# One step of a diffusion backbone layer on one Trainium2 core: the 16 by 16 triangular inverses of the scan move from VectorE to GpSimd

## The chip, the core and the metric

The kernel runs as one program on one core of a Trainium2 chip. Its time is the device time in microseconds (us). Before the change it is 2394.75 us, the median of three runs that lie between 2390.08 and 2395.71 us. The engines are written as in the profile: PE is TensorE, DVE is VectorE, ACT is ScalarE, POOL is GpSimd, SP is SyncE; a q behind a name is that engine's instruction queue, in which DMAs are issued.

## What is computed

One layer of a hybrid model over 1024 latent tokens and 256 context tokens of width 1024, all in float32. The token mixer has three branches: neighbourhood attention over an 8 by 16 window and the context, a bidirectional RWKV-7 scan, and a gated MLP over chunks of 128 positions. They are merged by sigmoid gates; then come an output projection, a normalisation, a SwiGLU feed-forward part and a second normalisation. The change touches only the scan:

```
def step(S, inp):
    r_t, w_t, k_t, v_t, kk_t, a_t = inp
    s_kk = jnp.einsum('...vk,...k->...v', S, kk_t)
    S = (S * w_t[..., None, :] - s_kk[..., :, None] * (kk_t * a_t)[..., None, :]
         + v_t[..., :, None] * k_t[..., None, :])
    return S, (jnp.einsum('...vk,...k->...v', S, r_t) if emit else None)
```

It runs in two directions, for 8 heads of width 64, over 1280 positions; the state after the context seeds the latent part.

## The kernel before

The scan is done in chunks of 64 positions. Inside a chunk the recurrence is a linear system with a 64 by 64 unit triangular matrix for each head and direction, and the kernel inverts these matrices ahead of the steps that use them.

The unit of work is called a block here. Block m (0 to 19, the list `L` at line 582) is one pair of heads, both directions, and four chunks of each, so that 16 matrices are inverted at once. Neighbouring blocks belong to two different pairs of heads; the state goes from block m to block m + 2. `rwkv_run` prepares blocks 0 and 1, then for each m runs the four rounds of `step` of block m (lines 744 to 785) and prepares block m + 2.

`prep` (line 626) loads a block's inputs, takes the exponentials `E` (L638, three buffers, so that the buffer of block m is free when the steps of block m - 3 are done; POOL sets the ones in it, L637), builds the factors `BK`, `KKe` and `KKo` on DVE (L643 to L649) and on POOL (L652, L653), multiplies them on PE (L662), transposes `BK` (L665) and masks the result into the triangular matrices `G` on DVE (L672, L673).

`invert` (line 691) writes `G` to DRAM (L697) and reads back the four 16 by 16 diagonal blocks of each of the 16 matrices, so that 64 small matrices lie on 64 partitions (`z`, tile gz, L699). POOL sets `Dm`, the first half of the tile DD, to the identity (L702, L703). Then comes the substitution: 15 steps, each a product into `tmp` (tile dtmp, L707) and an addition into `Dm` (L709). Step q works on 15 - q rows of q + 1 values, 15 to 64 values on each partition, 45.3 on average, and each instruction needs the one before it. L710 copies the transposed result into the second half of DD. DD goes to DRAM (L712) and comes back spread over 128 partitions as `Dc` (L714). DVE spreads it into block diagonal matrices `Db` and `Dt` (L730), and PE and DVE build the full inverse `X` from them in four rounds (tile ho, L725; L734, L739). gz, DD and dtmp have one buffer each. The steps of block m need its `X` at L763.

PE also has work that fills gaps: 28 projections of the input (`filling`, L543), 48 products of 128 by 512 each, written as L223, L224 and L225 with the tile d. They belong to the gates and to the queries and are called after the scan in the program. Here they are named fill products. Their weights are split on ACT (L211) and, in four pieces each, on POOL (L215).

No order is written out by hand around the change. All instructions are put into the queues of their engines when the program is built, by a scheduler that takes from the ready ones by priority, with a planned duration for each instruction. Each engine runs its queue strictly in order. So a fill product stands in PE's queue where the plan saw a gap, whether or not there is one on the chip.

Of the kernel before, what the change touches and what calls it, by code (L numbers as in the profile page):

```python
# [12 lines left out]
ALU = mybir.AluOpType  # L13
# [46 lines left out]
class Kern:  # L60
# [630 lines left out]
    def invert(self, jobs):  # L691
        nc, c = self.nc, self.c
        gs = self.dr.tile([16, 4160], F32, name="gs", tag="gs", bufs=2)
        for d, J in enumerate(jobs):
            for h in range(2):
                dst = bass.AP(gs.tensor, gs.offset + (8 * d + h) * 4160, [[64, 64], [8320, 4], [1, 64]])
                nc.scalar.dma_start(dst, J["G"][64 * h:64 * h + 64])  # L697
        z = self.T([64, 16, 16], "gz", 1)
        nc.sync.dma_start(z, bass.AP(gs.tensor, gs.offset, [[1040, 64], [64, 16], [1, 16]]))  # L699
        DD, tmp = self.T([64, 2, 16, 16], "DD", 1), self.T([64, 64], "dtmp", 1)  # L700
        Dm = DD[:, 0]
        nc.gpsimd.memset(Dm, 0.0)  # L702
        nc.gpsimd.memset(Dm.rearrange("p a b -> p (a b)")[:, 0:256:17], 1.0)  # L703
        for q in range(15):
            n, w = 15 - q, q + 1
            t = tmp[:, 0:n * w].rearrange("p (a b) -> p a b", b=w)
            nc.vector.tensor_tensor(t, z[:, q, q + 1:16].unsqueeze(2).to_broadcast([64, n, w]),  # L707
                                    Dm[:, q, 0:w].unsqueeze(1).to_broadcast([64, n, w]), ALU.mult)
            nc.vector.tensor_tensor(Dm[:, q + 1:16, 0:w], Dm[:, q + 1:16, 0:w], t, ALU.add)  # L709
        nc.vector.tensor_copy(DD[:, 1], Dm.rearrange("p a b -> p b a"))  # L710
        ds = self.dr.tile([2, 64, 256], F32, name="ds", tag="ds", bufs=2)
        nc.sync.dma_start(ds.rearrange("x p f -> p x f"), DD.rearrange("p x a b -> p x (a b)"))  # L712
        Dc = self.T([P, 16, 16], "Dc", 1)
        nc.sync.dma_start(Dc, bass.AP(ds.tensor, ds.offset, [[16, P], [2048, 16], [1, 16]]))  # L714
        bmb = c["bm"].rearrange("p (b t) -> p b t", t=16).unsqueeze(1).to_broadcast([P, 8, 4, 16])

        def blk(x):
            return x.rearrange("p u (b t) -> p u b t", t=16)

        def each(e, f):  # L720
            for u in range(8):
                for z in (0, 64):
                    q = slice(z, z + 64)
                    w, x = f(q, u)
                    nc.tensor.matmul(e[q, u, :], w, x, start=True, stop=True)  # L725

        Db, Dt, ET = (self.T([P, 8, 64], n, 1) for n in ("Db", "Dt", "ET"))
        X = self.T([P, 8, 64], "X", 2)
        for o, q in ((Db, 0), (Dt, 8)):
            nc.vector.tensor_tensor(blk(o), Dc[:, q:q + 8, :].unsqueeze(2).to_broadcast([P, 8, 4, 16]), bmb, ALU.mult)  # L730
        nc.scalar.activation(X, Dt, AF.Copy)
        e = self.ps.tile([P, 8, 64], F32, name="ho", tag="ho", bufs=1)
        each(e, lambda q, u: (jobs[u // 4]["G"][q, u % 4, :], Db[q, u, :]))
        nc.vector.tensor_tensor(ET, e, c["om"].unsqueeze(1).to_broadcast([P, 8, 64]), ALU.mult)  # L734
        src = Dt
        for t0 in (16, 32, 48):
            e = self.ps.tile([P, 8, 64 - t0], F32, name="ho", tag="ho", bufs=1)
            each(e, lambda q, u: (ET[q, u, :], src[q, u, t0:64]))
            nc.vector.tensor_tensor(X[:, :, t0:64], e, Dt[:, :, t0:64], ALU.add)  # L739
            src = X  # L740
        for d, J in enumerate(jobs):
            J["X"] = X[:, 4 * d:4 * d + 4]
# [724 lines left out]
```

## Time and profile before

| what | value |
|---|---|
| median of three runs | 2394.75 us |
| the profiled execution's own time | 2394.73 us |
| its span in the profile | 2392.9 us |
| PE busy | 2253.3 us, 94% |
| DVE busy | 1531.1 us, 64% |
| ACT busy | 895.3 us, 37% |
| POOL busy | 683.8 us, 29% |
| the scan, first L757 to last steps | 525.1 to 1097.5 us |
| DVE, ACT, POOL busy in it | 435.08, 233.28, 104.72 us |

The profile is one execution. A group's row has its line, engine, operation, output<-inputs, shape and count; then busy time and the mean of one in ns; then the idle time of the engine before it with what ended it. A timeline row has start, duration, engine, line and tiles, and in brackets the idle time before it. A wait row has total, times and longest. Each 64 by 64 product shows as two PE records, so x32 in a PE row are 16 products of the program.

### The profile page before, as it was taken

Reading aid. Unit: us, or ns where it says so; the run is one execution under the profiler, and the core shown is the slowest. Engines: PE = TensorE matmul, PEld = TensorE weight load, DVE = VectorE, ACT = ScalarE, POOL = GpSimd, SP = SyncE. Lnnn points to the kernel's source line nnn. Section 1 sums busy time; section 2 is a strip of 40 time slices with the busy share of each in tenths; the row PEclk is TensorE's granted clock in tenths of the full one; section 3 lists DMA queues with packets and bytes.
Section 4 is the critical chain, followed back from the end, with each engine's and each line's share of the span. In section 5 each row is a group of like instructions: output and inputs, shape, how many; then the busy total and the mean of one; then the engine's idle time right before and its main releaser. Section 6 shows DMA issues by size and latency. Waiting matters only on the chain.

```text
span 2392.9 us, 40066 instructions
## 1 busy us (share of the span) xinstructions
PE 2253.3 (94%) x15352; PEld 1790.2 (75%) x15352; DVE 1531.1 (64%) x3054; ACT 895.3 (37%) x1697; POOL 683.8 (29%) x708
## 2 busy tenths in 40 slices
PE   5899999998899998999999989999799999999997
PEld 4778888876677766667777768777588888877886
DVE  8885445437778777771676745686775555555835
ACT  4432425333344434343454532332533333332421
POOL 6221213441111121112312230333444333325402
PEclk9999999999999999899999999999799999999999
DMA  7676444545344444433865666464122222246541
GB/s 248 211 234 173 143 137 148 191 134 121 98 108 113 111 109 106 102 79 91 214 171 141 162 213 218 144 215 138 62 90 87 85 90 82 80 161 248 172 158 53
DMA packets 291861, 337.50 MB, mean 141 GB/s; under 512 B 140082, under 2 KB 210994, under 8 KB 291668
## 3 DMA queue, kind: packets, MB, share of 16 engines
q1 hardware_dynamic: 224548, 240.91, 34.6%
q10 hardware_dynamic: 54608, 51.40, 7.2%
q0 software_dynamic: 12512, 42.62, 4.9%
q8 instruction: 121, 1.98, 0.4%
q14 instruction: 72, 0.59, 0.1%
HBM read 248.85 MB, written 85.99 MB: 140 GB/s over the span
## 4 chain that ended last, share of the span: by engine, by line
PE 68%; DVE 16%; DMA 5%; issue 4%; ACT 4%; POOL 3%; SPq 0%; ACTq 0%; DVEq 0%; POOLq 0%
PE d L225 13%; PE d L223 13%; PE d L224 13%; PE ho L725 3%; PE pv L909 3%; PE d L1028 3%; PE d L1029 3%; PE d L1027 3%; PE gr L662 2%; PE pt L895 2%; DVE w L243 1%; DVE junk L243 1%; PE sc L771 1%; DVE DD L709 1%; DVE dtmp L707 1%
## 5 line engine op out<-in xcount | busy, mean ns | idle before, releaser
L225 PE MATMUL d<-hh,wl 128*128 128x512 f32 x1056 | 429.5, 407 | 0.0
L223 PE MATMUL d<-hh,wh 128*128 128x512 f32 x1056 | 428.8, 406 | 0.0
L224 PE MATMUL d<-hl,wh 128*128 128x512 f32 x1056 | 428.3, 406 | 0.0
L225 PEld LDWEIGHTS d<-hh,wl 128*128 128x128 f32 x1056 | 201.8, 191 | 46.8 <-issue 5.4
L224 PEld LDWEIGHTS d<-hl,wh 128*128 128x128 f32 x1056 | 201.7, 191 | 44.2 <-issue 3.4
L223 PEld LDWEIGHTS d<-hh,wh 128*128 128x128 f32 x1056 | 201.4, 191 | 43.2 <-issue 3.6
L215 DVE TENSOR_TENSOR wl<-wr,wh 128x1024 fp32r<-128x1024 f32 x51 | 65.0, 1274 | 159.8 <-ACT wh L211 111.5
L211 ACT ACTIVATE wh<-wr 128x1024 fp32r<-128x1024 f32 x79 | 83.5, 1057 | 191.8 <-PE d L224 149.1
L215 POOL TENSOR_TENSOR wl<-wr,wh 128x256 fp32r<-128x256 f32 x112 | 86.6, 803 | 225.3 <-ACT wh L211 211.7
L240 DVE TENSOR_TENSOR o<-wr,o 128x1024 fp32r<-128x1024 f32 (+1 forms) x64 | 92.5, 1447 | 20.3 <-ACT o L237 19.9
L1028 PE MATMUL d<-dl,ah 128*128 128x512 f32 x252 | 98.4, 391 | 2.8 <-DVE dl L240 2.8
L1029 PE MATMUL d<-dh,al 128*128 128x512 f32 x252 | 98.3, 390 | 0.1
L1027 PE MATMUL d<-dh,ah 128*128 128x512 f32 x252 | 98.2, 390 | 0.1
L237 ACT ACTIVATE o<-wr 128x1024 fp32r<-128x1024 f32 (+1 forms) x64 | 59.2, 926 | 100.0 <-PE d L224 73.9
L909 PE MATMUL pv<-pT,V 128*64 128x128 f32 (+2 forms) x640 | 93.5, 285 | 0.0
L240 DVE TENSOR_TENSOR al<-ar,ah 128x512 fp32r<-128x512 f32 x42 | 42.1, 1020 | 78.6 <-ACT ah L237 78.6
L1022 POOL TENSOR_TENSOR wl<-wr,wh 128x1024 fp32r<-128x1024 f32 x16 | 42.9, 2690 | 169.4 <-DVE wr L1020 124.3
L1255 POOL TENSOR_TENSOR act<-act 128x512 f32<-128x512 f32 x22 | 29.6, 1348 | 194.0 <-issue 160.1
L781 ACT ACTIVATE rv<-sc,E 64x64 f32<-64x64 f32 x152 | 38.9, 303 | 123.1 <-DVE rv L779 112.8
L662 PE MATMUL gr<-KKo,BK 64*128 64x128 f32 (+1 forms) x320 | 61.5, 313 | 24.3 <-DVE KKo L649 21.2
L909 PEld LDWEIGHTS pv<-pT,V 128*64 128x64 f32 (+2 forms) x640 | 69.2, 139 | 18.2 <-issue 13.0
L707 DVE TENSOR_TENSOR dtmp<-gz,DD 64x15 f32<-64x15 f32 (+2 forms) x300 | 70.6, 235 | 16.5 <-DMA gz<-gs 7.7
(397 smaller groups left out, 5878.7 us busy)
## 6 DMA issues: line engine op xcount, KB each, us to landing
wr<-wgu SPq DMA_DIRECT2D x45, 512.0 KB
dr<-wdn SPq DMA_DIRECT2D x42, 512.0 KB
wa<-wada SPq DMA_DIRECT2D x32, 512.0 KB
wr<-win SPq DMA_DIRECT2D x31, 512.0 KB
wr<-win ACTq DMA_DIRECT2D x28, 512.0 KB
s_gt<-stg ACTq DMA_DIRECT2D x48, 256.0 KB
wr<-wbr SPq DMA_DIRECT2D x24, 512.0 KB
g<-s_gt SPq DMA_DIRECT2D x48, 256.0 KB
```

Source lines behind the costliest of these rows:

```text
L211: nc.scalar.activation(hi[:, :n], raw[:, :n], AF.Copy)
L215: (lo_eng or self.lo_eng).tensor_tensor(lo[:, q], raw[:, q], hi[:, q].bitcast(F32), ALU.subtract)
L223: nc.tensor.matmul(ps, w, xh, start=first and k == 0, stop=False)
L224: nc.tensor.matmul(ps, w, xl, start=False, stop=False)
L225: self.last = nc.tensor.matmul(ps, lo[:, P * k:P * k + P], xh, start=False, stop=last and k == n - 1)
L240: (lo_eng or nc.vector).tensor_tensor(lo, src, hi.bitcast(F32), ALU.subtract)
L662: prev = nc.tensor.matmul(o[:, u, 0:W], x, y, start=True, stop=True)
L707: nc.vector.tensor_tensor(t, z[:, q, q + 1:16].unsqueeze(2).to_broadcast([64, n, w]), Dm[:, q, 0:w].unsqueeze(1).to_broadcast([64, n, w]), ...
L909: nc.tensor.matmul(o, V[0:k, vt, 64 * e:64 * e + 64], pt[0:k, i, :], start=(i == 0), stop=(i == len(cols) - 1))
L1027: nc.tensor.matmul(ps, xh, wh, start=first, stop=False)
L1028: nc.tensor.matmul(ps, xh, wl, start=False, stop=False)
L1029: nc.tensor.matmul(ps, xl, wh, start=False, stop=last)
```

## The change

The 15 products, the 15 additions and the transposed copy of each block go to POOL instead of DVE. Nothing else is edited.

```diff
@@ -704,10 +704,10 @@
         for q in range(15):
             n, w = 15 - q, q + 1
             t = tmp[:, 0:n * w].rearrange("p (a b) -> p a b", b=w)
-            nc.vector.tensor_tensor(t, z[:, q, q + 1:16].unsqueeze(2).to_broadcast([64, n, w]),
+            nc.gpsimd.tensor_tensor(t, z[:, q, q + 1:16].unsqueeze(2).to_broadcast([64, n, w]),
                                     Dm[:, q, 0:w].unsqueeze(1).to_broadcast([64, n, w]), ALU.mult)
-            nc.vector.tensor_tensor(Dm[:, q + 1:16, 0:w], Dm[:, q + 1:16, 0:w], t, ALU.add)
-        nc.vector.tensor_copy(DD[:, 1], Dm.rearrange("p a b -> p b a"))
+            nc.gpsimd.tensor_tensor(Dm[:, q + 1:16, 0:w], Dm[:, q + 1:16, 0:w], t, ALU.add)
+        nc.gpsimd.tensor_copy(DD[:, 1], Dm.rearrange("p a b -> p b a"))
         ds = self.dr.tile([2, 64, 256], F32, name="ds", tag="ds", bufs=2)
         nc.sync.dma_start(ds.rearrange("x p f -> p x f"), DD.rearrange("p x a b -> p x (a b)"))
         Dc = self.T([P, 16, 16], "Dc", 1)
```

The scheduler plans the whole program anew, and the queues of all engines change in the scan. POOL's queue around block 13, before: the preparation of block 13 (KKe_3984 to KKo_3989), a weight of a fill projection (wl), then the identity of block 13.

```order
297 L637 MEMSET E 128x4 x2
298 L652 TENSOR_TENSOR KKe_3984<-E,rl 64x4x64
299 L653 TENSOR_TENSOR KKo_3985<-E,rl 64x4x64
300 L652 TENSOR_TENSOR KKe_3988<-E,rl 64x4x64
301 L653 TENSOR_TENSOR KKo_3989<-E,rl 64x4x64
302 L215 TENSOR_TENSOR wl<-wr,wh 128x256 x4
303 L702 MEMSET DD 64x256
304 L703 MEMSET DD 64x16
```

POOL's queue now, from the identity of block 13 on; KKe_3992 to KKo_3997 and the E ahead of them are the preparation of block 14.

```order
710 L702 MEMSET DD 64x256
711 L703 MEMSET DD 64x16
712 L637 MEMSET E 128x4 x2
713 L707 TENSOR_TENSOR dtmp<-gz,DD 64x15
714 L709 TENSOR_TENSOR DD<-DD,dtmp 64x15
715 L707 TENSOR_TENSOR dtmp<-gz,DD 64x28
716 L652 TENSOR_TENSOR KKe_3992<-E,rl 64x4x64
717 L709 TENSOR_TENSOR DD<-DD,dtmp 64x14x2
718 L653 TENSOR_TENSOR KKo_3993<-E,rl 64x4x64
719 L707 TENSOR_TENSOR dtmp<-gz,DD 64x39
720 L652 TENSOR_TENSOR KKe_3996<-E,rl 64x4x64
721 L709 TENSOR_TENSOR DD<-DD,dtmp 64x13x3
```

The substitution of block 13 now stands behind the memset of E for block 14, and four instructions of that block's preparation stand inside it.

PE's queue before, from the last transposes of block 14's preparation to the first product of block 13 that needs `Db`.

```order
3514 L665 MATMUL gr<-c_ident,BK 128x128 x4
3515 L225 MATMUL d<-hh_577,wl 128x512
3516 L223 MATMUL d<-hh_626,wh 128x512
3517 L224 MATMUL d<-hl_627,wh 128x512
3518 L763 MATMUL sc<-rb_4000,X 64x64 x4
3519 L225 MATMUL d<-hh_626,wl 128x512
3520 L223 MATMUL d<-hh_251,wh 128x512
3521 L224 MATMUL d<-hl_252,wh 128x512
3522 L225 MATMUL d<-hh_251,wl 128x512
3523 L223 MATMUL d<-hh_290,wh 128x512
3524 L224 MATMUL d<-hl_291,wh 128x512
3525 L725 MATMUL ho<-Db,G 64x64 x16
```

The same place in PE's queue now.

```order
3423 L665 MATMUL gr<-c_ident,BK 128x128 x3
3424 L223 MATMUL d<-hh_290,wh 128x512
3425 L224 MATMUL d<-hl_291,wh 128x512
3426 L225 MATMUL d<-hh_290,wl 128x512
3427 L223 MATMUL d<-hh_341,wh 128x512
3428 L224 MATMUL d<-hl_342,wh 128x512
3429 L725 MATMUL ho<-Db,G 64x64 x16
```

Five fill products and no step product stand there now, where nine fill products and four step products stood. Counted over the whole queue, 768 fill products stand between the first L757 and the last L775 of the scan before, and 641 now; behind the attention's last product, 232 before and 350 now.

## The prediction

> **What bounds the kernel now.** I read the page first, for the chain that ended last.
>
> ```profile
> PE 68%; DVE 16%; DMA 5%; issue 4%; ACT 4%; POOL 3%; SPq 0%; ACTq 0%; DVEq 0%; POOLq 0%
> L707 DVE TENSOR_TENSOR dtmp<-gz,DD 64x15 f32<-64x15 f32 (+2 forms) x300 | 70.6, 235 | 16.5 <-DMA gz<-gs 7.7
> ```
>
> PE leads, and the substitution takes DVE some 141 us in all (L709 is a twin of L707). Next, busy time by stage, for the scan and for the end of the fill behind the attention.
>
> ```profile
> core 0: us, PE busy (x) PEld busy (x) DVE busy (x) ACT busy (x) POOL busy (x), PEclk, DMA share, GB/s
> 525.10:1097.50 572.40, 527.85 (x6965) 396.58 (x6966) 435.08 (x1335) 233.28 (x709) 104.72 (x208) 0.95 0.43 105
> 1397.20:1447.00 49.80, 45.03 (x198) 34.82 (x197) 13.16 (x16) 13.06 (x20) 16.84 (x15) 0.97 0.71 244
> ```
>
> PE looks full in the scan, but a matmul's record overlaps the next, so busy is not work. What PE waits for at the first round of the inverse (L725) says more.
>
> ```profile
>   DVE Db L730: 16.3, 19
> ```
>
> In 19 of 20 blocks PE stands there, 0.86 us each, until `Db` comes: the work planned ahead of L725 just fails to cover the inverse's latency. So I follow one block, number 13, on the timelines of PE, DVE and POOL.
>
> ```profile
> 879.44 0.66 PE L665 MATMUL gr<-c_ident,BK 128*128 128x128 f32 x4
> 890.10 0.17 DVE L707 TENSOR_TENSOR dtmp<-gz,DD 64x15 f32<-64x15 f32 x1 [0.39 <-DMA gz<-gs]
> 895.03 0.15 POOL L637 MEMSET E<- 128x4 f32 x2 [10.90 <-ACT rv L781]
> 896.25 0.68 POOL L653 TENSOR_TENSOR KKo<-E,rl 64x256 f32<-64x256 f32 x1
> 896.29 0.72 DVE L707 TENSOR_TENSOR dtmp<-gz,DD 64x64 f32<-64x64 f32 x1
> 904.76 0.37 DVE L710 COPY DD<-DD 64x256 f32<-64x256 f32 x1
> 913.02 1.15 PE L725 MATMUL ho<-Db,G 64*64 64x64 f32 x32 [0.33 <-DVE Db L730]
> 924.42 0.21 DVE L707 TENSOR_TENSOR dtmp<-gz,DD 64x64 f32<-64x64 f32 x1
> ```
>
> From the end of the transposes (880.1) to L725 (913.0) pass 32.9 us; 15.0 of them, 890.1 to 905.1, are substitution and copy. Their own work on DVE is 7.4 us (30 x 0.235 + 0.37); the rest is other DVE work that stands between. The substitution of a block, first product to end of copy, averages 16.2 us over the 20 blocks; these are the ends of the first and of the last.
>
> ```profile
> 532.47 0.17 DVE L707 TENSOR_TENSOR dtmp<-gz,DD 64x15 f32<-64x15 f32 x1
> 545.86 0.37 DVE L710 COPY DD<-DD 64x256 f32<-64x256 f32 x1
> 1068.91 0.15 DVE L707 TENSOR_TENSOR dtmp<-gz,DD 64x15 f32<-64x15 f32 x1
> 1079.13 0.39 DVE L710 COPY DD<-DD 64x256 f32<-64x256 f32 x1
> ```
>
> **The substitution on POOL.** No row shows this form on POOL. The nearest are a product of one element, of 256, a copy, and the gap before L653.
>
> ```profile
> L1370 POOL TENSOR_TENSOR st<-st 128x1 f32<-128x1 f32 x7 | 1.4, 194 | 0.5
> L652 POOL TENSOR_TENSOR KKe<-E,rl 64x256 f32<-64x256 f32 x32 | 22.6, 705 | 24.7 <-ACT E L638 16.3 <-ACT ub L764 4.5 <-DMA rl<-s_r 2.3
> L653 POOL TENSOR_TENSOR KKo<-E,rl 64x256 f32<-64x256 f32 x32 | 23.4, 732 | 2.3
> L571 POOL COPY KKe<-c_ident 64x256 f32<-64x256 f32 x6 | 2.4, 394 | 0.2
> ```
>
> L653's undisturbed 0.68 gives (0.68 - 0.194) / 255 = 1.9 ns an element, so an average instruction of 45.3 elements takes 0.28 us, and with a gap of 2.3 / 32 = 0.07 it costs 0.35. Bounds are 0.19 and 0.70, the two rows; I take 0.35, on the line between them. Thirty make 10.6 us, the copy 0.46, together 11.1. Four things are added or taken:
>
> - POOL's queue has 23 of L652/L653 and 5 of L215 inside substitutions, at some 0.76 us: 1.1 us a block.
> - At a head like block 13's the substitution waits for `E`: the memset ran at 895.03, 4.9 us after the data were there. Seven heads stand like this; I take 2 us for each, 0.7 a block (0 to 5).
> - POOL and DVE hold each other up. The 64-element product takes 0.21 us alone (924.42) and 0.72 beside POOL's L653 (896.29). After the change the DVE operations with two inputs in SBUF meet the substitution:
>
> ```profile
> L649 DVE TENSOR_TENSOR KKo<-E,kkl 64x256 f32<-64x256 f32 x40 | 23.2, 579 | 1.2
> L648 DVE TENSOR_TENSOR KKe<-E,kkl 64x256 f32<-64x256 f32 x40 | 22.3, 557 | 12.9 <-ACT E L638 10.9 <-issue 1.1 <-POOL E L637 0.8
> L646 DVE SCALAR_TENSOR_TENSOR BK<-bb,le 128x256 f32<-128x256 f32 x40 | 18.9, 472 | 0.6 <-DMA bb<-s_bb 0.5
> L643 DVE TENSOR_TENSOR BK<-kd,le 128x256 f32<-128x256 f32 x20 | 9.3, 467 | 0.7 <-DMA kd<-s_kd 0.5
> L645 DVE TENSOR_TENSOR BK<-kd,le 128x256 f32<-128x256 f32 x20 | 8.8, 442 | 0.2
> L730 DVE TENSOR_TENSOR Db<-Dc,c_bm 128x512 f32<-128x512 f32 x20 | 13.8, 688 | 13.1 <-DMA Dc<-ds 13.0
> L730 DVE TENSOR_TENSOR Dt<-Dc,c_bm 128x512 f32<-128x512 f32 x20 | 13.7, 683 | 0.0
> ```
>
> Their sum is 110 us, 5.5 a block; a substitution fills 12 of a block's 28.6 us (572.4 / 20), so 2.3 meet it, and half of that, 1.2, holds it up (0 to 5.5).
> - `Db` no longer queues behind another block's substitution: 0.3 less.
>
> That is 11.1 + 1.1 + 0.7 + 1.2 = 14.1 against 16.2, and 0.3: the latency falls by **2.4 us** (5.4 with nothing in the way).
>
> Behind a substitution that waits stand the next block's L652/L653 and the weights of L215 in POOL's queue, and PE's L662 and L225 wait for those. I cost this at nothing, since the same late inverse holds PE at L725 a little later anyway; where that doesn't cover it, four of L652/L653 are 4 x 0.75 = 3 us for each of the seven heads, 21 us.
>
> [...]
>
> **The cover in PE's queue.** The spacing of fill products comes from a run of 57.
>
> ```profile
> 1419.67 0.39 PE L223 MATMUL d<-hh,wh 128*128 128x512 f32 x1
> 1432.49 0.39 PE L225 MATMUL d<-hh,wl 128*128 128x512 f32 x1
> ```
>
> 12.82 us / 56 = 0.229 us. With it, 0.07 for a product of L725 (1.15 / 16), 0.165 for a transpose (0.66 / 4), and an estimated 0.10 to 0.15 for the small products of the steps and of L662 between these, the work between a block's last transpose and its L725 falls from 26.4 to 20.0 us on average (block 13: 27.8 to 19.8). At the scan's clock of 0.95 that is **6.7 us less cover**, while the latency falls by 2.4: PE stands 4.3 us longer for each block's inverse. Where the wait of the block before lies inside the same stretch it counts for both. That is so in 9 of 20 blocks of the new queue, so a block pays 4.3 / 1.45 = 2.97, and 20 blocks **59 us**.
>
> **The sum.** In the scan:
> - 127 fill products fewer (768 to 641): 127 x 0.229 / 0.95 = 30.6 us less work.
> - 59 us more waiting for the inverse.
> - The steps' DVE operations (L759, L765, L779) lose the substitution from their queue. PE's waits for their results:
>
> ```profile
> PEld sc L757 <- ACT rv L781: 13.7, 25, 1.7
> PEld sc L771 <- DVE ub L765: 11.7, 21, 2.5
> PEld sc L763 <- ACT rb L760: 11.6, 24, 1.4
> PE sc L757 <- ACT rv L781: 6.2, 11, 1.5
> ```
>
> They make 43 us; I take a quarter off, 11 us (0 to 43), since longer waits for the inverse hide the rest.
>
> So the scan goes from 572.4 to 572.4 - 30.6 + 59 - 11 = 590. Behind the attention 118 fill products more (232 to 350) at 0.229 cost 27 us, uncovered: PE is busy 45 of 49.8 us there with nothing but fill. The other 9 lie under the attention; I cost them at nothing, and at 2 us without that cover. DMAs, memsets and tiles stay as they are. In all 17.4 + 27 = **+44 us**. The profiled execution took 2394.73 us, as good as the median, so the forecast is **2439 us**. About 0.3%, 7 us, is what a measurement of this kernel can tell from no change.
>
> **The rivals.**
>
> *The scan gains what the plan expects.* The substitution runs on POOL undisturbed (latency 5.4 us less) and three quarters of the 43 us go. For it speaks that DVE loses a third of its work in the scan; against it, the instructions inside POOL's substitutions. Waits grow by (6.7 - 5.4) / 1.45 x 20 = 18: -30.6 + 18 - 32 + 27 = -18, **2377 us**, faster. It decides if substitution and copy stay near 11 us. Chance 0.14.
>
> *Work only moves.* Latency as there, the steps' gain as in my sum: -30.6 + 18 - 11 + 27 = +3, **2398 us**, no change that can be told. For it speaks that the number of PE's instructions doesn't change and the 27 us are paid in any case; against it the same as above. Chance 0.13.
>
> [...] All 5.5 us of the DVE operations hold up each substitution, and the ten operations on the way wait some 0.28 us each for POOL: the latency rises by 5.5 - 1.2 + 2.8 - 2.4 = 4.7. Waits grow by (6.7 + 4.7) / 1.45 x 20 = 157: -30.6 + 157 - 11 + 27 = +142, **2537 us**. For it speaks the 0.72 beside 0.21; against it, that only part of these operations falls into a substitution. [...] Chance 0.06.
>
> My own case has 0.67. That the change isn't made is no rival: POOL's queue shows the chain.
>
> **Range and chances.** My case's bounds: a latency that falls by 4 us (half of the additions gone) gives 37 us of waits, +22; one that falls by 0.3, for long waits behind `E`, gives 88, +73, and without the steps' gain +84. Reaching into the other cases until 2 in 10 are left out gives 2388 to 2485. Faster 0.14, same 0.13, slower 0.73.
>
> **What would show it.** In the profile after: L707 and L709 on POOL near 0.28 us, with 0.07 between; a block's substitution with copy near 14 us; PE's wait at L725 for `Db` several times 16.3 us; the scan near 590 us; the fill behind the attention near 77 us (49.8 + 27). The forecast is wrong if the wait at L725 stays near 16 us, or if the scan gets shorter by more than 27 us.

## The result, and the profile after

The changed kernel takes 2451.61 us, median of four runs (2435.70 to 2460.36), beside 2392.41 us for four runs of the kernel before: a ratio on record of 1.0232, with an interval of 1.0202 to 1.0262 (the two medians alone give 1.0247). The profiled execution is the fastest of the four, 2435.70 us; its granted clock has a mean of 0.967, and that of the other three 0.954 to 0.958. Against the profiled execution of before (2394.73 us) it is 41.0 us longer.

On the page, the substitution is on POOL now; these rows stand beside the row of L707 shown of before.

```profile
L707 POOL TENSOR_TENSOR dtmp<-gz,DD 64x15 f32<-64x15 f32 (+2 forms) x300 | 83.6, 279 | 97.2 <-DMA gz<-gs 75.9
L709 POOL TENSOR_TENSOR DD<-DD,dtmp 64x15 f32<-64x15 f32 (+2 forms) x300 | 87.2, 291 | 22.5
```

An instruction takes 0.285 us on the mean, and where none of them waits for gz the idle time ahead of one is (97.2 - 75.9 + 22.5) / 600 = 0.073 us. The copy, from the groups of POOL:

```profile
L710 POOL COPY DD<-DD 64x256 f32<-64x256 f32 x20 | 12.6, 632 | 1.3
```

Next the stages: scan, attention, and the fill products behind it. The rows give the stretch, its length, the busy time of PE, PE's weight loads, DVE, ACT and POOL, and the granted clock third from the end. First before, cut at the end of the last L775.

```profile
525.10:1118.60 593.50, 548.54 (x7162) 411.17 (x7161) 437.66 (x1344) 240.44 (x732) 108.13 (x214) 0.95 0.42 104
1118.60:1397.40 278.80, 268.94 (x1633) 213.29 (x1634) 183.14 (x567) 137.23 (x255) 66.85 (x49) 0.98 0.62 166
1397.40:1447.40 50.00, 45.23 (x198) 35.02 (x199) 13.36 (x16) 13.36 (x20) 16.84 (x15) 0.97 0.70 243
```

The same stages after:

```profile
524.80:1139.30 614.50, 517.58 (x7035) 395.57 (x7034) 307.24 (x724) 235.54 (x729) 280.08 (x824) 0.91 0.39 96
1139.30:1414.30 275.00, 267.55 (x1642) 212.42 (x1643) 179.74 (x567) 136.40 (x255) 68.65 (x53) 0.99 0.63 171
1414.30:1487.60 73.30, 70.65 (x313) 55.72 (x314) 12.66 (x16) 18.33 (x27) 21.66 (x23) 1.00 0.56 199
```

The scan is 21.0 us longer, the attention 3.8 shorter, the tail 23.3 longer; with 0.5 elsewhere these are the 41.0 us. (The prediction cut the scan of before at 1097.5, inside the last block's inverse; the last step ends at 1118.6.) In the scan PE is busy 31.0 us less, and yet the scan is longer: PE stands more, and its clock is lower (0.91, where it was 0.95). What it stands for, in the table of waits (us in total, times, longest), before:

```profile
PE gr L662 <- DVE KKo L649: 21.2, 16, 2.3
PE sc L757 <- ACT rv L781: 6.5, 12, 1.5
PE ho L725 <- DVE Db L730: 5.9, 6, 2.6
PE sc L771 <- DVE ub L765: 4.2, 4, 2.1
PE sc L763 <- ACT rb L760: 3.5, 5, 1.2
PE gr L662 <- POOL KKo L653: 0.4, 1, 0.4
```

And after:

```profile
PE ho L725 <- DVE Db L730: 61.2, 15, 7.6
PE gr L662 <- POOL KKo L653: 24.4, 10, 6.1
PE gr L662 <- DVE KKo L649: 7.0, 7, 2.3
PE sc L763 <- ACT rb L760: 2.5, 2, 2.2
PE sc L757 <- ACT rv L781: 0.5, 2, 0.3
PE sc L771 <- DVE ub L765: 0.3, 1, 0.3
```

The wait for `Db` grew by 55.3 us, that at L662 by 24.0 - 14.2 = 9.8, and the steps' waits fell by 10.9: 54.2 us more. Block 13 again, whose rows stand in the prediction:

```profile
904.13 0.15 POOL L637 MEMSET E<- 128x4 f32 x2 [10.20 <-ACT rv L781]
904.23 0.21 POOL L707 TENSOR_TENSOR dtmp<-gz,DD 64x15 f32<-64x15 f32 x1
906.14 0.80 POOL L653 TENSOR_TENSOR KKo<-E,rl 64x256 f32<-64x256 f32 x1
916.18 0.55 PE L665 MATMUL gr<-c_ident,BK 128*128 128x128 f32 x3
917.82 0.60 POOL L710 COPY DD<-DD 64x256 f32<-64x256 f32 x1
924.00 0.69 DVE L730 TENSOR_TENSOR Db<-Dc,c_bm 128x512 f32<-128x512 f32 x1 [7.09 <-DMA Dc<-ds]
924.75 0.48 PE L725 MATMUL ho<-Db,G 64*64 64x64 f32 x4 [6.87 <-DVE Db L730]
```

The substitution starts late behind the memset of `E`, runs past the point at which PE has used up its queue (917.9), and PE stands 6.87 us where it stood 0.33.

**Scan, split in three.** For the experiments I split the scan, from the first L662 to the last L775, with the timeline of PE and the records of the granted clock: time without any product (idle), half of the busy time at half clock (an estimate of what the clock cost: in the traces of before and after, fill products follow each other every 0.43 us at half clock and every 0.23 at full clock), and the rest (PE's work at full clock). Each row is of one profiled execution: that of the changed kernel is the fastest of its four, that of e7 the slowest of its six (2466.77 us).

| kernel | scan | work | idle | clock |
|---|---|---|---|---|
| before | 605 | 526 | 48 | 32 |
| after | 625 | 485 | 100 | 41 |
| e5, engine alone | 611 | 522 | 42 | 47 |
| e6, plan alone | 634 | 483 | 83 | 68 |
| e1, engine and old order on PE | 716 | 518 | 117 | 80 |
| e2, DVE and new order on PE | 686 | 481 | 128 | 77 |
| e3b, short substitution, new plan | 558 | 488 | 45 | 25 |
| e7, products in the holes | 646 | 506 | 72 | 69 |
| e4b, L652 on DVE, new plan | 620 | 484 | 85 | 51 |
| e8, 18 operations on DVE, old plan | 633 | 524 | 60 | 50 |
| e11, engine alone, L652 on DVE | 574 | 528 | 34 | 11 |
| e12, L652 on DVE alone | 606 | 528 | 50 | 27 |

The work is that of the order: 518 to 528 us with the old one, 481 to 488 with the new (506 with e7's added 25). Everything else is idle time and clock.

### The profile page after: what moved, and what is told of

Same layout as the page of the kernel before. It is cut to its first block, busy times and chain, and to the rows that moved or that the text cites. A ratio compares the mean times of both kernels' runs of the same rounds, so it can differ in the third digit from the quotient of the medians.

```text
span 2433.7 us, 40095 instructions
## 1 busy us (share of the span) xinstructions
PE 2246.9 (92%) x15352; PEld 1795.4 (74%) x15352; DVE 1394.7 (57%) x2434; ACT 892.4 (37%) x1697; POOL 861.9 (35%) x1328
## 5 line engine op out<-in xcount | busy, mean ns | idle before, releaser
L215 DVE TENSOR_TENSOR wl<-wr,wh 128x1024 fp32r<-128x1024 f32 x51 | 64.9, 1273 | 190.1 <-ACT wh L211 141.7
L215 POOL TENSOR_TENSOR wl<-wr,wh 128x256 fp32r<-128x256 f32 x112 | 84.5, 782 | 241.9 <-ACT wh L211 165.8
L707 POOL TENSOR_TENSOR dtmp<-gz,DD 64x15 f32<-64x15 f32 (+2 forms) x300 | 83.6, 279 | 97.2 <-DMA gz<-gs 75.9
L709 POOL TENSOR_TENSOR DD<-DD,dtmp 64x15 f32<-64x15 f32 (+2 forms) x300 | 87.2, 291 | 22.5
L662 PE MATMUL gr<-KKo,BK 64*128 64x128 f32 (+1 forms) x320 | 61.4, 312 | 34.0 <-POOL KKo L653 24.4
L725 PE MATMUL ho<-Db,G 64*64 64x64 f32 x640 | 30.4, 263 | 61.3 <-DVE Db L730 61.2
```

What stands on the lines that cost most here:

```text
L215: (lo_eng or self.lo_eng).tensor_tensor(lo[:, q], raw[:, q], hi[:, q].bitcast(F32), ALU.subtract)
L707: nc.gpsimd.tensor_tensor(t, z[:, q, q + 1:16].unsqueeze(2).to_broadcast([64, n, w]), Dm[:, q, 0:w].unsqueeze(1).to_broadcast([64, n, w]), ...
L709: nc.gpsimd.tensor_tensor(Dm[:, q + 1:16, 0:w], Dm[:, q + 1:16, 0:w], t, ALU.add)
```

## The experiments

The theory: the loss is in the new plan, which puts 6.7 us less work ahead of L725 and moves 118 fill products behind the attention, while the latency falls by only 2 to 3 us. The main rival: the substitution on POOL costs by itself, through what it does to DVE and to POOL's queue. To part the two I held queues: at the end of the build each instruction of an engine gets an order-only edge (no wait) to the one ahead of it in the queue of the other kernel.

```diff
+def keep_order(tc, nc):
+    t = {i.name: i for i in nc.cur_bb.bb.instructions}
...
+            i = t.get(f"I-{at + int(d) + k}")
...
+                x = last.get(i.engine)
...
+                    tc.add_manual_dep(i, x.name, no, reason="keep_order")
+                last[i.engine] = i
```

**PE's order held, the rest planned anew.** Edit of e1 to the changed kernel, of e2 to the kernel before, with PE alone in the table:

```diff
         Kern(tc, aps).build()
+        pe_order(tc, nc)
```

> The changed kernel with all of PE's instructions held to the order they have in the kernel before (11778 places alike), substitution and copy on POOL; the other engines' orders are left to the scheduler. Theory (cover): the loss comes from PE's order, planned with 6.7 us less work ahead of L725 than before, while the latency fell by only 2 to 3 us. With the old cover back, PE's wait at L725 for Db falls from 122 us to below the 16 us of before, the tail behind the attention is 50 us again, and the steps keep their relief of some 11 us: 2392 - 11 - 10 = 2371 us, at most 2392. [...] Rival (tail): only the 118 fill products behind the attention cost, so 2452 - 27 = 2425 us.

> The kernel before, substitution and copy on DVE, with all of PE's instructions held to the order of the changed kernel. Theory (cover): the latency is that of before and the cover is 6.7 us shorter, so waits at L725 grow by 6.7 / 1.45 x 20 = 92 us over before, 31 us of fill leave the scan and 27 us come back behind the attention: 2392 + 92 - 31 + 27 = 2480 us, slower than the change itself. Rival (engine): with the chain back on DVE the time is back at 2392 to 2400 us. Rival (tail): 2392 + 27 = 2419 us.

Measured: e1 2498.5 us, ratio 1.0445 (1.0418 to 1.0472); e2 2507.1 us, 1.0494 (1.0456 to 1.0532). Both are slower than the change itself. For e1 the theory was wrong by over 100 us and the tail rival by 73; a cost of the substitution on POOL by itself, the main rival, was left standing. e2 came 27 us above the theory's 2480, and far above both of its rivals. PE's waits in e1:

```profile
PE gr L662 <- POOL KKo L653: 40.3, 10, 5.7
PE gr L662 <- DVE KKo L649: 33.1, 8, 7.3
```

`Db` is not among the late things any more; the next block's preparation is. In e1's POOL queue 22 of the 64 L652 and L653 stand inside a substitution and the others behind whole substitutions of 30 instructions, and a substitution at the queue's head waits for gz 216 us in all (75.9 in the changed kernel). Whether that was POOL or the new plan of the other queues, e1 cannot say, since holding PE had made the scheduler plan them anew.

**All five queues held.** The same edit with the instructions of all engines in the table: e5 is the engine without the plan, e6 the plan without the engine.

> The engine change without the new plan: substitution and copy on POOL, and the instructions of all five engines held to the order in which the kernel before issues them, the substitution merged into POOL's queue at the places that it has in the plan of before. It asks what held e1_chain_pool_old_order at 2498 us, where only PE was held and the other queues were planned anew (PE waited at L662 for KKo of L653 on POOL, 40 and 72 us). Theory (cover): with the old cover and old queues the shorter latency is left over: 2371 to 2392 us. Rival (POOL's queue): L652 and L653 of the next block stand behind a substitution that waits for gz, PE waits for them at L662, and the old cover makes this worse, not better, since in the old order L662 of the next block is ahead of L725: 2430 us or more, with waits at L662 over 60 us.

> The new plan without the engine change: substitution and copy on DVE, and the instructions of all five engines held to the order in which the changed kernel issues them, the substitution merged into DVE's queue at the places that it has in that plan. Theory (cover): PE's wait at L725 grows as in e2_chain_dve_new_order, which came to 2507 us with the other queues planned anew: 2480 to 2507 us. Rival: part of e2's time is from the other queues being planned anew around a PE order that did not suit them; with all queues as in the changed kernel it takes 2452 us like that, the engine makes no difference.

Measured: e5 2395.17 us, 0.9995 (0.9965 to 1.0025); e6 2446.90 us, 1.0208 (1.0168 to 1.0248). This separates them. The engine alone costs nothing that can be told, the plan alone costs 2.1%, against 2.3% for both. The rival of e5 fails (e1's time came from its other queues). In e6 the rival's 2452 us is the right one, and the theory's 2480 to 2507 is out. So the theory holds as to the cause, but not in two of its numbers. In e5 no gain is left over: first product to end of copy is 16.3 us a block on POOL with the old queues, where DVE took 16.2. POOL's other work inside it is 3.3 us a block, 2.1 of them L652 and L653; in the changed kernel it is 1.1. And in e6 it is 10.4 us on DVE, where the changed kernel takes 12.9 on POOL; yet the time is nearly the same. PE's waits in e6:

```profile
PE sc L771 <- DVE ub L765: 25.2, 18, 4.5
PE gr L662 <- DVE KKo L649: 23.2, 14, 4.0
PE sc L763 <- ACT rb L760: 11.6, 10, 2.3
PE sc L757 <- ACT rv L781: 7.1, 5, 2.7
```

`Db` is in time there (3 us of waiting), but the substitution stands in one piece in DVE's queue, ahead of the steps' operations, and PE stands for those. With less work planned in between, something is late; the engine decides which.

**Latency alone.** The substitution stops after 8 of 15 steps; e3 holds PE to the changed kernel's order, e3b all five engines.

```diff
-        for q in range(15):
+        for q in range(8):
```

> The changed kernel, PE in the changed kernel's own order, but the substitution stops after 8 of its 15 steps (16 POOL operations a block where there were 30; the last seven rows of every 16x16 inverse are left incomplete). Theory (cover): the latency falls by 14 x 0.36 = 5.0 us a block, and by the 1.45 of the prediction 5.0 / 1.45 x 20 = 69 us of waits go: 2452 - 69 = 2383 us, PE's wait at L725 near 50 us. Rival (engine by what it holds up, or tail): the wait at L725 only covers others, so that what goes there comes back at the steps or at L662: 2440 us or above.

> The changed kernel with the substitution stopped after 8 of its 15 steps (the last seven rows of every 16x16 inverse are left incomplete), and the instructions of all five engines held to the changed kernel's order, where e3_short_chain_new_order held PE alone. Theory (cover): 5.0 us less latency, 69 us less waiting: 2383 us, and no more waits at the steps than in the changed kernel. Rival (the steps take over): PE's waits at L763 and L771 grow as they did in e3 (18 to 57 us at L771), since the substitution was only the first of two late things: 2420 to 2435 us.

Measured: e3 2427.3 us, 1.0143 (1.0114 to 1.0172); e3b 2371.87 us, 0.9914 (0.9886 to 0.9941). With all queues held, time falls by as much as the theory's 69 us: (1.0232 - 0.9914) x 2392 = 76 us. The wait for `Db`:

```profile
PE ho L725 <- DVE Db L730: 21.2, 13, 2.9
```

The substitution became 5.7 us shorter (12.2 to 6.5, first to last of its operations), so a us of latency is worth 76 / 20 / 5.7 = 0.67 us a block, one part in 1.5. The prediction's 1 in 1.45 is another thing, since it counts waits alone. By the table the idle time fell by 55 us, one part in 2.1, of which the wait for `Db` is 40 us, and the clock gave 16 more. In e3 the freshly planned queues gave 24 us of waits at L771 and 12 at L763, and over two thirds of the gain were lost. The rival of e3b described e3's queues, not the kernel.

**Work in the holes.** Ten products ahead of L725 in the 11 blocks where PE stood longest, all queues held.

```diff
+        self.nb = getattr(self, "nb", -1) + 1
+        for _ in range(10 if self.nb in (1, 2, 3, 5, 7, 9, 12, 13, 15, 17, 19) else 0):
+            x = self.xs(0)[0][0]
+            nc.tensor.matmul(e.rearrange("p a b -> p (a b)"), x[:, 0:P], x, start=True, stop=True)
         each(e, lambda q, u: (jobs[u // 4]["G"][q, u % 4, :], Db[q, u, :]))
```

> The changed kernel, all five engines held to its order, with work added and none removed: 10 products of 128x512 (2.29 us of PE at the full clock) directly ahead of the first product of L725 in the 11 blocks where PE stood 2.4 to 7.6 us at that place (blocks 1, 2, 3, 5, 7, 9, 12, 13, 15, 17 and 19). They write what L725 then overwrites. Theory (cover): the holes at L725 are real idle time on the path, so 11 x 2.29 / 0.91 = 28 us of added work cost nothing: 2452 us, up to 10 us either way. If PE's idle time is also what lowered the granted clock of the scan from 0.95 to 0.91, the time even falls, by up to 20 us. Rival (no holes, only waits of a queue that is full anyway): the work is added to the time, 2452 + 28 = 2480 us.

Measured: 2452.59 us, 1.0233 (1.0195 to 1.0271), the time of the changed kernel: 25 us of work for nothing, and the rival's 2480 is outside the interval. PE's wait for `Db` fell from 61.2 to 35.4 us. Whether the clock rose stays open. In the profiled scans it is 0.88 in e7 and 0.91 in the changed kernel, but these are the slowest and the fastest of their runs; the mean clock of whole runs is 0.962 to 0.972 in the six of e7 and 0.954 to 0.967 in the four of the changed kernel.

**What lies inside the substitution.** L652 and L653 go to DVE: e4 (PE held to the new order), e4b (all held to the new plan), e11 (all held to the old plan, substitution on POOL), e12 (all held to the old plan, substitution on DVE).

```diff
-            nc.gpsimd.tensor_tensor(KKe[0:64, :, 128:192], ee[0:64], rr[0:64], ALU.mult)
-            nc.gpsimd.tensor_tensor(KKo[64:128, :, 64:128], ee[64:128], rr[64:128], ALU.mult)
+            nc.vector.tensor_tensor(KKe[0:64, :, 128:192], ee[0:64], rr[0:64], ALU.mult)
+            nc.vector.tensor_tensor(KKo[64:128, :, 64:128], ee[64:128], rr[64:128], ALU.mult)
```

> The changed kernel, PE in the changed kernel's own order, L652 and L653 on DVE instead of POOL, so that POOL's queue holds little but the substitution. By the prediction's terms 1.1 us of interleaved operations and part of the 1.2 us of lock go, at most some 1.8 us a block: 1.8 / 1.45 x 20 = 25 us, 2427 us. Rival (POOL's queue costs beyond the latency): PE's waits at L662 for KKo of L653 (59 us after, 19 before) go as well, some 40 us more: 2390 us. Rival (neither binds): DVE's 64 more operations of 0.57 us take the gain, 2445 to 2460 us.

> The changed kernel with L652 and L653 on DVE at their places in the plan, all five engines held to its order (e4_L652_on_dve_new_order held PE alone and came to 2466 us). In the changed kernel 23 of these 64 operations, 16.4 us in all, lie inside substitutions, 0.82 us a block, and PE waited 24 us at L662 for L653. Theory (cover): 0.82 / 1.45 x 20 = 11 us less at L725 and up to 24 us less at L662: 2417 to 2441 us. Rival (e4's result was the operations themselves, not the new plan): 2460 us or above.

> As e5_engine_alone (substitution and copy on POOL, all five engines held to the order of before), with L652 and L653 on DVE at their places in that plan. In e5 56 of the 64 lay inside substitutions, 41.3 us, 2.1 us a block, so that the substitution took 15.3 us on POOL where it takes 12.2 in the changed kernel. Theory (cover): the latency falls by 2.1 us, PE's 20 us of waits at L725 for Db go, and the kernel beats both: 2370 to 2382 us. Rival (what is taken off POOL comes back on DVE, at the steps): 2390 to 2400 us.

> The control for e11_L652_on_dve_old_order (2368 us, 0.988): the kernel before with L652 and L653 on DVE, substitution and copy left on DVE, all five engines held to the order of before. Theory (e11's gain is the substitution on a POOL that has nothing else in between, which takes 12.7 us there, and the steps' DVE operations that no longer stand behind it): DVE gets 64 operations of 0.47 us, 1.5 us a block, more, a part of which lies between the parts of the substitution and ahead of the steps' operations: 2395 to 2420 us. Rival (the gain is the move of L652 and L653 alone, from POOL's 0.72 us to DVE's 0.47 us): 2368 to 2380 us as in e11.

Measured: e4 2466.21 us, 1.0307 (1.0278 to 1.0336), more than even its last rival had; e4b 2438.15 us, 1.0179 (1.0139 to 1.0219), in the theory's range: 13 us less than the change, though the two intervals just overlap; e11 2368.02 us, 0.9878 (0.9846 to 0.9911); e12 2393.88 us, 1.0011 (0.9993 to 1.0028). So e11 beats both kernels, the one before by 1.2%, and neither of its parts does it alone: the substitution on POOL (e5) and L652 on DVE (e12) change nothing that can be told. Together the substitution takes 12.7 us on POOL, first to last operation, where it took 15.3 in e5. The rest is argued from the theory: the steps' operations have DVE, and the old plan has the work that covers the latency. PE's largest waits in e11:

```profile
PE gr L662 <- DVE KKo L649: 11.5, 12, 2.0
PE ho L725 <- DVE Db L730: 10.5, 7, 3.6
```

The row of e11's scan, with the clock at 0.98:

```profile
515.60:1089.10 573.50, 539.70 (x7213) 405.00 (x7213) 334.91 (x800) 243.62 (x742) 247.23 (x777) 0.98 0.45 112
```

By the table above, 14 of the 32 us that the scan gains against before are idle time, 20 are the clock, and the work is 2 more.

**A shorter substitution on DVE.** Two 8x8 halves in common steps, then the corner; all queues held to the old plan.

```diff
...
+        for q in range(7):
...
+            nc.vector.tensor_tensor(Dd[:, :, q + 1:8, 0:w], Dd[:, :, q + 1:8, 0:w], t, ALU.add)
...
+            nc.vector.tensor_tensor(t, l.unsqueeze(2).to_broadcast([64, 8, 8, 8]),
+                                    r.rearrange("p q b -> p b q").unsqueeze(1).to_broadcast([64, 8, 8, 8]), ALU.mult)
+            nc.vector.tensor_reduce(o, t, axis=AX.X, op=ALU.add)
```

> The kernel before with another substitution, on DVE, with the same result: the two 8x8 halves of each 16x16 block in 7 common steps, the corner by two products of 8x8 matrices, 18 operations where there were 30. All five engines held to the order of before, the 18 at the first 18 places of the 30. Estimate from rows: 14 x 0.235 + 4 x 0.69 (the 128x512 operation of L730) = 6.1 us of DVE, where it was 7.1, and up to 3 us less latency, since 12 places with other work between them go. Theory (cover): the cover of before just suffices, so little of it counts: 6 us of PE's waits at L725 and a part of the steps' 43 us, 2375 to 2388 us. Rival (latency is on the path of before too): 3 / 1.45 x 20 = 41 us less, 2351 us. Rival (the 512-element operations cost more than the row says): 2393 us or above.

Measured: 2422.19 us, 1.0110 (1.0080 to 1.0140): slower, as the last rival had it. The groups of DVE:

```profile
L717 DVE TENSOR_TENSOR dtmp<-DD,dtmp 64x512 f32<-64x512 f32 x20 | 22.5, 1124 | 0.4
L719 DVE TENSOR_REDUCE dtmp<-dtmp 64x64 f32<-64x512 f32 x20 | 13.5, 675 | 0.5
```

The reduction costs what the estimate said, the product 1.12 in place of 0.69 us. DVE still works less on it than before (6.6 us a block against 7.1), so this alone does not explain the loss, 28 us in the scan. PE hardly waits for `Db`; idle and clock grew by 12 and 18 us, with a little more waiting at each of the steps and at L662. That the four long operations, in one piece, hold up the steps' operations is plausible, but was not tried.

## Why the prediction came out right, step by step

- **The operations on POOL.** 0.28 and 0.07 us were said; 0.285 and 0.073 came. From 15 to 63 elements the medians of the shapes rise by 1.7 ns an element; 1.9 was said. The copy took 0.63 where 0.39 was taken from a copy without transposition.
- **What is added.** Interleaved operations: 1.0 us a block (12 of L653, 11 of L652, 5 of L215: 20.0 us), 1.1 was said. What DVE cost POOL is hidden in the mean of 0.285: 34 of the 600 instructions took 0.1 to 0.8 us more than the median of their shape, each beside one of the DVE operations that the prediction lists (at 551.39 a product of 15 elements took 0.71 us beside the L730 of `Db`). Over the medians that is 0.7 us a block, where 1.2 was said. That half of what meets is held up was the author's estimate, and no run shows a lock, as the expectation of e4 names it. What the trace shows is this: of 78 instructions beside the listed operations 34 took longer, and of 293 beside other DVE operations alone none took more than 0.01 us over its median. For anything else inside, 12.2 - 8.6 - 1.0 - 30 x 0.073 = 0.4 us is left. Block 13 did wait behind `E`: from the issue of the read of gz to the first product passed 8.6 us, but in the other 19 blocks 2.6 to 5.6. First product to end of copy took 12.9, not 14.1. From the last `G` to the end of `Db` it fell from 32.5 to 30.3 us, 2.1 less, where 2.4 was said.
- **The cover.** Waits for the inverse: +59 said, +55.3 measured. From a block's last transposes to its L725 PE was busy for 28.9 us on average before and 21.7 after, 7.2 us less, where 6.7 was said; it stood there for 2.7 us before and 7.4 after, 4.7 more, where 4.3 was said. Twenty times 4.7 is 95 us, and the wait grew by one part in 1.7 of it, where the prediction took 1.45. So two small misses of size cancelled. The quoted row of before was misread, though: its 16.3 us in 19 times count PE's products (5.9 us, 6 times) and its weight loads (10.4, 13) as waits of their own. PE stood 0.3 us a block, not 0.86, in 6 blocks of 20. The cover did suffice, but in the blocks where PE didn't stand `Db` was at most 0.8 us ahead of it. That is why a sum of differences could still hold: with more to spare, part of the lost cover would have cost nothing.
- **Fill products and steps.** Busy time in the scan fell by 31.0 us (30.6 said); the waits at the steps by 10.9 (11 said). Both are luck in part. PE's work at full clock fell by 41, of which 127 x 0.229 = 29 are the products; 12 us have no name, and the lower clock took 9 back. The 43 us at the steps added weight loads to products, like the row of L725: PE's own waits there were 14.2 us, and three quarters of them went, not one.
- **POOL's queue.** L662 behind the substitution was costed at nothing. It grew by 24.0 us, 14.2 of which another wait there gave back. This term was too small by about 10 us; e1 shows how large it gets.
- **The tail.** 27 said, 23.3 measured.
- **The sum.** +17.4, 0 and +27 were said, +21.0, -3.8 and +23.3 measured: +44 against +41.0 in the profiled execution. That execution is the fastest of four, so the match is better than the forecast: 2439 us was 13 us under the median. The other 16 us of the median go with a lower clock in the other runs, of which no trace was kept; the clock was not in the sum.
- **One reason did not hold.** The latency was said to fall by 2.4 us because of POOL. It fell because of the plan, which puts less in between. From the last `G` to the end of `Db` pass 32.9 us with the engine alone (e5) and 27.7 with the plan alone (e6), beside 32.5 before and 30.3 after. For the substitution itself POOL takes 2.5 us more than DVE in the new plan (12.9 and 10.4) and as much in the old (16.3 and 16.2). The new plan was the cause of the loss, and e5 and e6 show it; in the changed kernel its lost cover is seen as the wait at L725.

The rivals: "the scan gains what the plan expects" and "work only moves" needed a latency that falls by 5.4 us, and the rival of 2537 us one that rises by 4.7; it fell by 2.1.

## What to carry to other kernels

When a change goes through a scheduler, ask what it plans for the changed instructions and what work it will take away because of that; here the engine alone cost nothing that can be told, and the plan alone cost 2.1%. Hold all queues to part the two, never one, since the rest is planned anew around it (e1 and e5 differ by 103 us with the same engine and the same PE queue). And look at what stands inside the chain on its new engine: with L652 and L653 among it the move gained nothing (e5), with them elsewhere 1.2% (e11).

## What the runs showed of the hardware

**Most holes on PE were paid twice.** In block 13 of the changed kernel PE stands from 917.9 to 924.8; windows around it, with PE's busy time first and the granted clock third from the end:

```profile
919.90:921.40 1.50, 0.00 (x0) 0.00 (x0) 0.00 (x0) 0.00 (x0) 0.42 (x3) 0.97 0.70 182
921.40:923.00 1.60, 0.00 (x0) 0.00 (x0) 0.00 (x0) 0.00 (x0) 1.60 (x4) 0.50 0.70 109
926.40:928.20 1.80, 1.80 (x17) 1.47 (x15) 1.76 (x5) 1.00 (x3) 0.00 (x0) 0.51 0.60 182
928.20:930.00 1.80, 1.80 (x36) 1.35 (x35) 0.15 (x1) 0.00 (x0) 0.00 (x0) 1.00 0.67 162
```

The clock falls to half inside the hole and stays there for 3.4 us of work after it. In this scan 14 of 15 holes over 2.5 us are followed by half clock, 1.8 to 5.1 us after their start; in e1 20 of 23. The stretches at half clock in the scans of before and after last 3.41, 6.83 or 10.24 us, that is 3.41 us or a multiple of it. In e7, 48.2 us in 12 holes over 2.5 us are left of 73.4 us in 15, and all 12 were followed by half clock.

Ten of the 12 stretches of before have no such hole ahead of them. The scans of all 14 traces, cut into pieces of 3.41 us where the clock's changes lie, show what they follow. Of 2082 pieces at full clock, all 132 in which PE was busy for less than 45% were followed by half clock, and none of the 1520 in which it was busy for 90% or more; between these it went either way. The 12 stretches of before follow pieces in which PE was busy for at most 82%, so there several short waits within one piece did what a hole did. Back to full clock it went 213 times, each time after a piece in which PE was busy for at least 87%. What isn't explained is how long a stretch lasts, since 126 pieces with 97% and more stayed at half clock: 3.4 to 10.2 us in the changed kernel, up to 20.5 in e7, and 27.3 in e5 after a hole of 3.2.

**The clock, not only the wait, is what kernels with the same products differ by.** With the products of the old order (7213 records), PE is busy 539.7 us in e11's scan at a clock of 0.98. The row of e1's scan:

```profile
513.20:1228.80 715.60, 598.51 (x7213) 451.01 (x7213) 315.36 (x736) 244.56 (x744) 285.69 (x841) 0.86 0.36 90
```

At 0.86 the same products keep it busy 598.5 us. In the changed kernel a sum at one fixed clock, as in the prediction, left out 9 us of the scan. Idle time alone does not fix the clock, though: e5 stands less than before (42 and 48 us) and loses more to it (47 and 32).
